# A transformer step on one core: the first feed-forward in seven half products, its adaLN vectors on TensorE

## The chip, the core and the metric

The kernel runs on one core of a Trainium2 chip. Its metric is the device time of one execution in microseconds (us). A core has five engines that run apart from each other: TensorE (PE in the profile, with PEld for its weight loads), VectorE (DVE), ScalarE (ACT), GpSimd (POOL) and SyncE (SP, which here only issues DMAs). Matmuls read SBUF and write PSUM, which has eight banks of 512 fp32 columns.

## What is computed

640 tokens (512 latent, 128 context) of width D = 1024 pass two layers. Layer 0 mixes tokens by neighbourhood attention, layer 1 by a gated linear recurrence (LRU); each is followed by a SwiGLU feed-forward of width 2816. Before every mixer and feed-forward stands an RMS norm with adaLN shift and scale, behind it a gated residual; these are six vectors per layer, for latent and context tokens each.

```python
def _adaln(cond, w_mod, b_mod):
    m = jax.nn.silu(cond) @ w_mod + b_mod            # 1024 x 6144 per layer
    return jnp.split(m, N_MOD, axis=-1)

def _modulate(x, g, shift, scale):
    return _rms_norm(x, g) * (1 + scale[:, None, :]) + shift[:, None, :]

def _swiglu(x, w_gu, w_down):
    gate, up = jnp.split(x @ w_gu, 2, axis=-1)
    return (jax.nn.silu(gate) * up) @ w_down
...
    ctx = ctx + g1_c[:, None, :] * o_c
    lat = lat + g1_l[:, None, :] * o_l
    f_c = _swiglu(_modulate(ctx, norm_g[i, 1], sh2_c, sc2_c), ffn_w_gu[i], ffn_w_down[i])
    f_l = _swiglu(_modulate(lat, norm_g[i, 1], sh2_l, sc2_l), ffn_w_gu[i], ffn_w_down[i])
    ctx = ctx + g2_c[:, None, :] * f_c
    lat = lat + g2_l[:, None, :] * f_l
```

## The kernel before

Activations lie transposed in SBUF: 8 blocks `k` of 128 features by 640 tokens. A product in fp32 precision is made of three fp32r matmuls: weights and activations are split into a high part (`whi`, `whx`, made by ScalarE's copy) and the rest (`wlo`, `wlx`, VectorE's difference), and hi·hi, hi·lo and lo·hi are added up in one PSUM bank. The function `some` issues them, L221 to L223, 24 for one output block of 128 features and one chunk of tokens (two chunks of 320, `CH`; 384 and 256, `CHL`, in the closing projections). Weights come by SP's DMA queue in pieces of 512 KB (`raw`).

The program is written once, and a scheduler that simulates the engines (`schedule_with_timeline_sim=True`) sets the order of each engine's instructions, within what tiles, pools (a tile waits until the buffer's earlier user is done) and pins (`issue_after`) allow. On the chip every engine then runs its own order and waits on semaphores.

The stages in order:

- `start`: the norm, the first two adaLN vectors and the first products of attention. The adaLN vectors are made on TensorE: with SiLU(cond) as 128 x 32 stationary block (`csp`, 2 columns used), four matmuls of 256 columns write four groups of 32 partitions of one bank (`ss`); the copied row is then turned into columns by matmuls with `sel`. `keep` issues dummy fp32 matmuls of 256 columns.
- `attn`: eight head pairs; `softmax` uses two PSUM banks `tp` for transpositions, two `sp` and one `op`. PE also gets products of the next pair, and the output projection's first ones.
- `ffn0`: the output projection of attention (`project` with `wo`), the moment (L540, L543) and the spread of its root (L557) of the norm, and `ffn`: for each of 22 columns of 128 features a gate and an up product, 2 x 2 chunks x 24 matmuls; the shift is a 2-column extra in one chunk (322 columns); after 8, 7 and 7 columns the down product, last in `project_closing`, which makes the LRU's input while it runs.
- `lru`, then `ffn1`: `project_halves` with `wlo`, and `ffn_halves`. Here x is kept in DRAM (`xd`), and the SBUF of x holds the normed activations as four blocks B11, B12, B21, B22 (half of the features by half of the tokens). Three columns are `plain`, the other 19 take gate and up products together by a Strassen form: seven products of 4 blocks x 3 matmuls x 320 columns (L1079 to L1081, in `product`), from sums of weights (`sum_weights`, POOL) and of activations (`sums`). The last down product is `project_last`.

The other ten adaLN vectors come from `modulations`, a generator of steps: `mod_cols` loads 128 rows of `w_mod` (512 KB, `mraw`, two buffers, POOL's DMA queue) and has VectorE multiply and add them up against `csb`, twice per load (L250, 1024 elements each). `fill(n)` takes n steps, at most the phase's `quota`; 24 are taken in attention and 56 in `ffn0`. `need` takes steps until a vector is there.

Of the kernel before, what the change touches and what calls it, by code (L numbers as in the profile page):

```python
# [36 lines left out]
FG = (1, 1, 1)  # L37
# [14 lines left out]
def _lay(inp):  # L52
# [30 lines left out]
    def tiles(w):  # L83
# [10 lines left out]
        "wm": wm.reshape(2, D, 6, D).transpose(0, 2, 3, 1).reshape(12, KT, P, D)[2:],  # L94
# [31 lines left out]
class _Step:  # L126
# [25 lines left out]
    def phase(self, name, **tags):  # L152
        with self.tc.tile_pool(name="ps" + name, bufs=1, space=bass.MemoryType.PSUM, reuse_waits="tile") as self.pp, \
                self.tc.tile_pool(name=name, bufs=1, reuse_waits="tile") as self.sb:
            self.wx, self.quota = [tags.pop(t, 0) for t in ("wx", "quota")]
            self.ptags, self.pbufs, self.share = list(tags), tags, True
# [139 lines left out]
    def start(self, hi, lo, sp, big):  # L296
# [5 lines left out]
        csp = self.t([P, KT, 32], F32, "csp", 1, sp)  # L302
# [91 lines left out]
        dve(nc.vector.tensor_scalar, v, aux[:, 256:256 + NT], 1.0 / D, EPS, ALU.mult, ALU.add)  # L394
# [5 lines left out]
        vectors(0, pm, 1, 1)  # L400
        row = rows(0, pm)
# [40 lines left out]
        keep(2)  # L442
# [109 lines left out]
    def spread(self, moment):  # L552
        nc = self.nc
        t0, bl, dg = moment
        ps = self.ps("rr" if "rr" in self.ptags else "mx")
# [35 lines left out]
    def project(self, w, hi, lo, gk, nxt=None, done=None, ahead=False):  # L591
        G = self.need(self.gcols, gk)
        for f in range(KT):
            u = self.unit(w[f], "m" if ahead else None)
            for t0, t1 in CH:
                self.residual(f, t0, t1, self.chunk(u, hi, lo, t0, t1, not ahead or f > 1), G, nxt)
                if nxt:
                    self.scale(f, t0, t1, *nxt)
            if done:
                done(f)  # L600
        if nxt:
            self.stats()
            self.shift(*nxt)

    def project_closing(self, w, hi, lo, gk, key, nh, nl, xd):
        G = self.need(self.gcols, gk)
        A, B = [self.need(self.AB, key + (j,)) for j in range(2)]
        us = []

# [4 lines left out]
        def normed(k, t0, t1):  # L614
            v = self.t([P, 384], F32, "nv", 3, self.sb)
# [3 lines left out]
        for f in range(KT):  # L619
            us.append(self.unit(w[f]))  # L620
            for c, (t0, t1) in enumerate(CHL):
                if c == 0 or f < KT - DEH:
                    out(f, t0, t1)
# [857 lines left out]
```

## Time and profile before

| | us |
|---|---|
| device time, median of 3 runs | 1521.38 (1519.66 to 1524.26) |
| device time of the profiled execution | 1522.34 |
| its span, first to last instruction | 1520.6 |
| PE busy | 1491.0 |
| DVE busy | 1062.4 |
| ACT busy | 697.9 |
| POOL busy | 253.2 |

The span is what the trace covers; the profiled execution's device time is 1.7 us more. Times in the trace count from the span's start. Matmuls overlap: one of 320 columns lasts 312 ns in the trace while the next starts some 147 ns after it, so a matmul's price in a full stretch is the distance of starts, not its duration. fp32 matmuls (not fp32r) stand as two entries each. The first feed-forward runs from about 372 to 863 us, the second from 1068 to 1510 us.

### The profile page before, as it was taken

The page shows a single profiled execution, that of the slowest core. Times are in us where ns is not written, and L with a number is a line of the kernel's source. Part 1 is how long each engine was busy: PE and PEld are TensorE (multiplying, and loading weights), DVE is VectorE, ACT ScalarE, POOL GpSimd, SP SyncE. Part 2 cuts the span into 40 slices and gives each one's busy share as a digit, 9 for nine tenths or more (in the row PEclk, how much of TensorE's full clock was granted, in tenths as well). Part 3 has the DMA queues.
Part 4 walks back from the last instruction along what each step waited for, and adds up shares of the span by engine and source line. Part 5 has one row for each costly group of instructions (what it writes and reads, how often), then busy time and mean ns, then how long its engine had stood idle before and what let it go on. Part 6 is the DMA issues. An engine that isn't in the chain of part 4 may idle for free. (4 is left out here: it accounts for less than half of the span.)

```text
span 1520.6 us, 26091 instructions
## 1 busy us (share of the span) xinstructions
PE 1491.0 (98%) x10359; PEld 1443.9 (95%) x10359; DVE 1062.4 (70%) x2005; ACT 697.9 (46%) x1268; POOL 253.2 (17%) x276
## 2 busy tenths in 40 slices
PE   8999999899999999999999999999999999999997
PEld 6999999899999999999999888899999999999997
DVE  5778998769999987434443769985965656566555
ACT  4576666754332123312321478864634342434243
POOL 0112132100111110000000114220322323222211
PEclk9999999999999999999999999999999999999999
DMA  9545665336566664222222443335342231323211
GB/s 379 165 142 162 188 188 172 117 136 187 179 190 197 207 195 134 62 84 84 65 64 92 145 131 109 119 104 175 97 125 83 71 111 56 100 67 98 70 56 70
DMA packets 72330, 196.65 MB, mean 129 GB/s; under 512 B 8048, under 2 KB 24592, under 8 KB 72080
## 3 DMA queue, kind: packets, MB, share of 16 engines
q1 hardware_dynamic: 57392, 142.32, 29.7%
q0 software_dynamic: 14240, 51.98, 11.2%
q8 instruction: 81, 1.33, 0.4%
q10 hardware_dynamic: 576, 0.68, 0.1%
q14 instruction: 41, 0.34, 0.1%
HBM read 179.48 MB, written 8.92 MB: 124 GB/s over the span
## 5 line engine op out<-in xcount | busy, mean ns | idle before, releaser
L221 PE MATMUL mm<-big,whi 128*128 128x320 f32 (+3 forms) x1233 | 383.7, 313 | 6.5 <-ACT big L1307 5.3
L222 PE MATMUL mm<-big,whi 128*128 128x320 f32 (+3 forms) x1233 | 383.7, 312 | 0.4 <-DVE big L564 0.2
L223 PE MATMUL mm<-big,wlo 128*128 128x320 f32 (+3 forms) x1233 | 383.9, 312 | 0.0
L221 PEld LDWEIGHTS mm<-big,whi 128*128 128x128 f32 x1233 | 232.8, 189 | 9.2 <-ACT big L1307 6.0
L222 PEld LDWEIGHTS mm<-big,whi 128*128 128x128 f32 x1233 | 233.3, 189 | 2.8 <-DVE big L1309 0.7
L223 PEld LDWEIGHTS mm<-big,wlo 128*128 128x128 f32 x1233 | 232.9, 189 | 1.5
L250 DVE SCALAR_TENSOR_TENSOR mprod<-mraw,csb 128x1024 f32<-128x1024 f32 x160 | 195.1, 1219 | 12.3 <-DMA mraw<-in_wm 11.8
L587 DVE SCALAR_TENSOR_TENSOR x<-mm,G,x 128x320 f32<-128x320 f32 (+2 forms) x192 | 77.9, 436 | 83.7 <-PE mm L223 83.5
L180 ACT CAST whi<-raw 128x1024 fp32r<-128x1024 f32 (+1 forms) x71 | 73.9, 1041 | 108.6 <-PE mm L222 62.4
L182 DVE TENSOR_TENSOR wlo<-raw,whi 128x1024 fp32r<-128x1024 f32 (+1 forms) x87 | 106.0, 1219 | 21.6 <-ACT whi L180 12.5
L221 PE MATMUL mm<-big,whx 128*128 128x320 f32 (+3 forms) x348 | 108.3, 311 | 0.0
L223 PE MATMUL mm<-big,wlx 128*128 128x320 f32 (+3 forms) x348 | 108.0, 310 | 0.0
L222 PE MATMUL mm<-big,whx 128*128 128x320 f32 (+3 forms) x348 | 107.8, 310 | 0.0
L246 POOL DMA_DIRECT2D mraw<-in_wm x80 | 43.1, 538 | 364.8 <-DVE mprod L250 270.5
L221 PE MATMUL mx<-big,whi 128*128 128x320 f32 (+3 forms) x287 | 89.4, 311 | 0.0
L223 PE MATMUL mx<-big,wlo 128*128 128x320 f32 (+3 forms) x287 | 89.1, 311 | 0.0
L222 PE MATMUL mx<-big,whi 128*128 128x320 f32 (+3 forms) x287 | 88.9, 310 | 0.0
L221 PE MATMUL mx<-big,whx 128*128 128x320 f32 (+3 forms) x260 | 80.6, 310 | 0.0
L223 PE MATMUL mx<-big,wlx 128*128 128x320 f32 (+3 forms) x260 | 80.5, 310 | 0.0
L180 ACT CAST whx<-raw 128x1024 fp32r<-128x1024 f32 (+1 forms) x40 | 41.1, 1029 | 85.5 <-PE mm L222 47.9
L222 PE MATMUL mx<-big,whx 128*128 128x320 f32 (+3 forms) x260 | 80.3, 309 | 0.0
L1307 ACT CAST whi<-raw 128x1024 fp32r<-128x1024 f32 (+1 forms) x41 | 41.3, 1008 | 73.2 <-PE mm L222 44.9
(347 smaller groups left out, 3721.5 us busy)
## 6 DMA issues: line engine op xcount, KB each, us to landing
raw<-in_gu SPq DMA_DIRECT2D x88, 512.0 KB, 3.5
mraw<-in_wm POOLq DMA_DIRECT2D x80, 512.0 KB, 3.9
raw<-in_dn SPq DMA_DIRECT2D x24, 512.0 KB, 3.6
sw<-in_wm SPq DMA_DIRECT2D x16, 512.0 KB, 10.7
raw<-in_wqk SPq DMA_DIRECT2D x16, 512.0 KB, 5.0
raw<-in_wi SPq DMA_DIRECT2D x16, 512.0 KB, 3.6
whi<-in_wi POOLq DMA_DIRECT2D x16, 512.0 KB, 4.1
raw<-in_dn SPq DMA_DIRECT2D x16, 448.0 KB, 3.3
```

What stands on the lines that cost most here:

```text
L180: nc.scalar.copy(hi, raw)
L182: nc.vector.tensor_tensor(lo, raw, hi.bitcast(F32), ALU.subtract)
L221: nc.tensor.matmul(ps, hi[:, k], xhi[:, k, s], start=(k == 0), stop=False)
L222: nc.tensor.matmul(ps, hi[:, k], xlo[:, k, s], start=False, stop=False)
L223: self.done = nc.tensor.matmul(ps, lo[:, k], xhi[:, k, s], start=False, stop=(k == last)).ins
L246: nc.gpsimd.dma_start(w, self.i["wm"][l * 6 + j - 2, f])
L250: nc.vector.scalar_tensor_tensor(prod, w, 1.0, self.csb[:, s], ALU.mult, ALU.mult, accum_out=out[:, s, f:f + 1])
L587: self.nc.vector.scalar_tensor_tensor(xs, ps[:, a - t0:b - t0], G[:, s, f:f + 1], xs, ALU.mult, ALU.add)
L1307: self.nc.scalar.copy(hi, v)
```

## The change

The first feed-forward takes the second one's code. `layer_end` is the old end of the program as a function, called for both layers: x is loaded, `project_halves` projects (for layer 0 its first five chunks as they come, `ahead`), writes x to DRAM and makes the four blocks, `ffn_halves` runs 3 plain columns and 19 in seven half products; its last down product is `project_closing` for layer 0, with weights loaded two at a time, chunk by chunk, and `project_last` for layer 1. `ffn` and `project` are gone.

Of the ten later adaLN vectors the first three stay on VectorE. The other seven are `mod_product`: 8 pieces of 512 KB each (`mraw`, two buffers, now on SP's queue), each with four 256-column matmuls into four groups of 32 partitions of one bank (L291), then a copy of the row, two matmuls that turn it (L297), and one addition that gives gate, shift or scale. Steps are taken by `fill` in `plain` and, three per column, in `ffn_halves`. In the start stage seven more dummies are issued, and the norm's sums are written 32 columns wide.

```diff
-FG = (1, 1, 1)
+FG = 3
...
     def modulations(self):
         yield from self.mod_gate(0, 2)
         yield from self.mod_ss(0, 3, 1)
-        yield from self.mod_gate(0, 5)
-        yield from self.mod_ss(1, 0, 0)
-        yield from self.mod_ss(1, 3, 1)
-        yield from self.mod_gate(1, 2)
-        yield from self.mod_gate(1, 5)
+        vecs = [(0, 5), (1, 1), (1, 0), (1, 2), (1, 4), (1, 3), (1, 5)]
+        srcs = [self.i["wmp"][l * 6 + j - 5, k] for l, j in vecs for k in range(KT)]
+        ahead = []
+
+        def piece():
+            while srcs and len(ahead) < 2:
+                w = self.t([P, D], F32, "mraw", 2, self.sb)
+                self.nc.sync.dma_start(w, srcs.pop(0))
+                ahead.append(w)
+            return ahead.pop(0)
+        for l, j in vecs:
+            yield from self.mod_product(l, j, piece)
+
+    def mod_product(self, l, j, piece):
+        nc = self.nc
+        ps = self.ps()
+        for k in range(KT):
+            w = piece()
+            for g in range(4):
+                nc.tensor.matmul(ps[32 * g:32 * g + 32, 0:256], self.csp[:, k], w[:, 256 * g:256 * g + 256], start=(k == 0), stop=(k == KT - 1))
+            if k < KT - 1:
+                yield
+        row = self.t([P, 256], F32, "row", 1, self.sb)
+        nc.scalar.copy(row, ps[:, 0:256])
+        for c in range(2):
+            nc.tensor.matmul(ps[:, 256 + 8 * c:264 + 8 * c], row[:, c * P:c * P + P], self.ident.rearrange("p (g c) -> p g c", g=4)[:, :, 0:2], start=True, stop=True)
...
+        nc.vector.tensor_tensor(out.rearrange("p s (g c) -> p s g c", c=2), ps[:, 256:272].rearrange("p (c g s) -> p s g c", c=2, g=4), b, ALU.add)
...
         pm = self.ps("ss")
+        keep(2)
         vectors(0, pm, 0, 0)
+        keep(2)
         vectors(0, pm, 0, 1)
         for j, b in enumerate(blocks):
-            pe(aux[:, 256 + j:257 + j], self.ssq[:, b:b + P], self.ones[:, 0:1], start=True, stop=True)
+            pe(aux[:, 288 + 32 * j:320 + 32 * j], self.ssq[:, b:b + P], self.ones[:, 0:32], start=True, stop=True)
...
         vectors(0, pm, 1, 1)
+        keep(2)
         row = rows(0, pm)
...
-        keep(2)
+        keep(3)
         normed(0)
...
-    def project_halves(self, w, hi, lo, gk, key, xd):
+    def project_halves(self, w, hi, lo, gk, key, xd, ahead=False):
...
+        if ahead:
+            for n, (f, t0, t1) in enumerate(early):
+                out(f, t0, t1, self.chunk(us[f], hi, lo, t0, t1, n > 2))
+            early = []
...
                 n += 1
+                self.fill(c or n > 2)
...
                 if f < PLAIN:
                     continue
+                self.fill(FG)
...
-        with self.phase("ffn0", at=2, rr=1, mx=2, wx=2, quota=56) as fp:
-            self.project(i["wo"], ohi, olo, (0, 2), ((0, 1), xhi, xlo), None, True)
...
-            self.ffn(0, xhi, xlo, fp, last)
+        mpool.close()
+        xd, xe = [dram.tile([D, NTOK], F32, tag=n, name=n) for n in ("xd", "xe")]
+        self.layer_end(xpool, i["x"], ohi, olo, i["wo"], 0, xd, True,
+                       lambda w, hi, lo, gk: self.project_closing(w, hi, lo, gk, (1, 0), xe))
...
-        with self.phase("ffn1", at=1, mx=3, mc=1, wx=2) as fp:
+        with self.phase(f"ffn{l}", at=1, mx=3, mc=1, wx=2, quota=0 if l else 56) as fp:
...
-            self.project_halves(i["wlo"], yhi, ylo, (1, 2), (1, 1), xd)
+            self.project_halves(w, hi, lo, (l, 2), (l, 1), xd, ahead)
```

Three places show how PE's order changes. In the rows a line number is that of each kernel's own file: L221 to L223 before are L222 to L224 after, L1079 to L1081 are L1067 to L1069, the moment's L540 and L543 are L576 and L579, the spread's L557 is L593; a number behind a name tells apart tiles of one tag, and the last figures are the output's size.

First, PE at the end of attention's output projection, ahead of the first feed-forward. Before, the projection's last product into an `mx` bank is followed by the moment of the norm:

```order
L221 MATMUL mx_4750<-big_4092,whx_4715 128x320
L222 MATMUL mx_4750<-big_4093,whx_4715 128x320
L540 MATMUL at_4673<-ones_72,ssq_4141 128x128
L540 MATMUL at_4691<-ones_72,ssq_4141 128x128
L543 MATMUL at_4691<-ones_72,sq_4635 128x128
L540 MATMUL at_4691<-ones_72,ssq_4141 128x128
L543 MATMUL at_4691<-ones_72,sq_4635 128x128
```

After:

```order
L224 MATMUL mm_4634<-big_3856,wlo_4399 128x320
L291 MATMUL tp_3201<-mraw_4839,csp_78 32x256 x4
L291 MATMUL tp_3201<-mraw_4872,csp_78 32x256 x4
L291 MATMUL tp_3201<-mraw_4906,csp_78 32x256 x4
L291 MATMUL tp_3201<-mraw_4939,csp_78 32x256 x4
L291 MATMUL tp_3201<-mraw_5021,csp_78 32x256 x4
L291 MATMUL tp_3201<-mraw_5054,csp_78 32x256 x4
L297 MATMUL tp_3201<-ident_63,row_5106 128x8 x2
L222 MATMUL mx_4294<-big_3856,whx_4290 128x320
L223 MATMUL mx_4294<-big_3857,whx_4290 128x320
```

Six pieces of the vector (0, 5) and its turn have come in between two products of the projection. The tile `tp` they add up in was taken in attention, from head pair 5 on: the step that `need` takes there to finish the third vector begins the fourth. Its bank is one of the two `tp` banks of attention and, in `ffn0`, the second `mx` bank.

Second, PE inside the first feed-forward, at the change from one product to the next. Before (`mx` and `mm` are banks of gate and up products):

```order
L223 MATMUL mx_5934<-big_4711,wlo_5931 128x320
L221 MATMUL mx_5934<-big_4711,whi_5930 128x320
L222 MATMUL mx_5934<-big_4712,whi_5930 128x320
L223 MATMUL mx_5934<-big_4711,wlo_5931 128x320
L221 MATMUL mm_5960<-big_4711,whi_5930 128x320
L222 MATMUL mm_5960<-big_4712,whi_5930 128x320
L223 MATMUL mm_5960<-big_4711,wlo_5931 128x320
L221 MATMUL mm_5960<-big_4711,whi_5930 128x320
```

After, in the seven half products (`mx_5623` and `mx_5774` are the accumulated halves of two columns):

```order
L1069 MATMUL mx_5623<-big_4722,wlx_5667 128x320
L291 MATMUL at_5610<-mraw_5750,csp_78 32x256 x4
L1068 MATMUL mx_5774<-big_4104,whi_5770 128x320
L1069 MATMUL mx_5774<-big_4104,wlo_5771 128x320
L291 MATMUL at_5610<-mraw_5756,csp_78 32x256 x4
L1067 MATMUL mx_5774<-big_4104,whi_5770 128x320
L1068 MATMUL mx_5774<-big_4104,whi_5770 128x320
L1069 MATMUL mx_5774<-big_4104,wlo_5771 128x320
```

Single pieces stand between fp32r matmuls, at 39 places in all for the last six vectors: 27 with one piece or part of one, 12 with two.

Third, PE at the spread of the norm's root ahead of the first feed-forward (`rr` before, a bank `mx` after). Before, 44 rows behind the moment:

```order
L222 MATMUL mm_4816<-big_4093,whi_4779 128x320
L223 MATMUL mm_4816<-big_4092,wlo_4780 128x320
L221 MATMUL mm_4816<-big_4092,whi_4779 128x320
L557 MATMUL rr_4686<-dg_4684,ones_72 128x128 x3
L222 MATMUL mm_4816<-big_4093,whi_4779 128x320
L223 MATMUL mm_4816<-big_4092,wlo_4780 128x320
```

After:

```order
L579 MATMUL at_4468<-ones_72,sq_4464 128x128
L576 MATMUL at_4468<-ones_72,ssq_4165 128x128
L579 MATMUL at_4468<-ones_72,sq_4464 128x128
L593 MATMUL mx_4481<-dg_4479,ones_72 128x128 x3
L222 MATMUL mx_4486<-big_3856,whi_4135 128x320
L223 MATMUL mx_4486<-big_3857,whi_4135 128x320
```

The spread now stands directly behind its moment.

More of the change, by code (lines that the diff above doesn't have):

```diff
@@ L589, in residual, with project_closing @@
             self.square(f, t0, t1)
[L591 to L605, printed above, removed]
+    def project_closing(self, w, hi, lo, gk, key, xd):
         G = self.need(self.gcols, gk)
@@ L608, in project_closing @@
         us = []
+        for f in range(0, KT, 2):
+            us += self.two(w[f:f + 2], f % 4)
+        nh, nl = self.nh, self.nl = [self.big(n=NTOK + 2) for _ in range(2)]
         def out(f, t0, t1):
@@ L619, in project_closing @@
         for f in range(KT):
[L620 to L623, printed above, removed]
-        for c, (t0, t1) in enumerate(CHL):
-            for f in range(KT - DEH, KT) if c else ():
-                out(f, t0, t1)
-                j = f - KT + DEH
-                for k in range(max(0, 2 * j - 2), 2 * j) if f < KT - 2 else ():
+            out(f, *CHL[0])
+        self.stat(*CHL[0])
+        for f in range(KT):
+            out(f, *CHL[1])
+            if 2 < f < KT - 1:
+                for k in range(2 * f - 6, min(2 * f - 4, 6)):
                     normed(k, *CHL[0])
-            for k in (6, 7) if c else ():
-                normed(k, *CHL[0])
-            self.stat(t0, t1)
+        for k in (6, 7):
+            normed(k, *CHL[0])
+        self.stat(*CHL[1])
         for k in range(KT):
@@ L998, in sums @@
         t2 = self.t([P, HT], F32, "c22", 2, self.sb)
-        nc.vector.tensor_tensor(b11, b12, b11, ALU.subtract)
+        with self.pin(self.halved):
+            nc.vector.tensor_tensor(b11, b12, b11, ALU.subtract)
         nc.vector.tensor_tensor(t2, b22, b11, ALU.subtract)
```

92 lines of the change are left out of this document (32 added, 60 removed).

## The prediction

> **What bounds the kernel now.** I read the page's first lines first: which engine fills the span.
>
> ```profile
> span 1520.6 us, 26091 instructions
> ...
> PE 1491.0 (98%) x10359; PEld 1443.9 (95%) x10359; DVE 1062.4 (70%) x2005; ACT 697.9 (46%) x1268; POOL 253.2 (17%) x276
> ```
>
> TensorE is busy for 98% of it. That share is pipelined, so I next cut the span into stages: window, then busy us and instructions of PE, PEld, DVE, ACT and POOL, then granted clock, DMA share and GB/s.
>
> ```profile
> 16.00:20.00 4.00, 3.16 (x26) 2.40 (x19) 1.13 (x4) 1.56 (x2) 1.19 (x1) 0.70 1.03 420
> 20.00:24.00 4.00, 4.00 (x16) 3.34 (x14) 2.49 (x8) 1.70 (x3) 0.00 (x0) 0.50 1.03 413
> 290.00:300.00 10.00, 5.83 (x44) 5.09 (x44) 7.99 (x14) 9.50 (x18) 1.69 (x3) 0.71 0.38 109
> 290.00:326.00 36.00, 29.90 (x246) 27.11 (x245) 23.56 (x64) 22.53 (x50) 2.29 (x5) 0.91 0.27 86
> 396.00:846.00 450.00, 450.00 (x3054) 450.00 (x3053) 292.72 (x532) 120.23 (x224) 25.33 (x47) 1.00 0.42 129
> 846.00:870.00 24.00, 21.04 (x137) 19.64 (x136) 19.00 (x53) 13.62 (x33) 2.04 (x9) 1.00 0.38 116
> 1068.00:1116.00 48.00, 46.24 (x309) 45.82 (x308) 42.19 (x78) 27.35 (x63) 13.24 (x9) 0.96 0.35 104
> 1116.00:1486.00 370.00, 369.74 (x2506) 368.79 (x2505) 218.16 (x348) 140.74 (x227) 99.79 (x72) 1.00 0.27 82
> ```
>
> The reader is to see two saturated stretches: 396 to 846 (first feed-forward) and 1116 to 1486 (second). They make one matmul per 450/3054 = 0.1473 us and per 370/2506 = 0.1476 us, nearly all with 320 columns. There is no idle PE time in the first, so there the count of PE work alone sets the time. The list of waits for PE alone (who waited for what: us in total, times, longest) names the two stalls that the prediction uses:
>
> ```profile
> PE at L540 <- DVE ssq L527: 1.7, 1, 1.7
> PE mm L1137 <- DVE xt L1309: 1.8, 1, 1.8
> ```
>
> VectorE's adaLN products in that stretch:
>
> ```profile
> 396.00:846.00 450.00, 111.66 (x182) 1.00 0.42 129
> ```
>
> These 111.7 us of VectorE go away, but VectorE is busy 292.7 of 450 us and no PE wait stands in the stretch: their removal is worth nothing by itself. What it buys is room for the weight sums.
>
> **The change, part by part.** The sum is made on PE time and taken against the profiled span of 1520.6 us (device time 1522.3; the three other runs have the median 1521.4, 0.9 us below it). Three runs spread over 0.3%, about what can be told from no change.
>
> *Seven half products.* Of 22 columns, 3 stay plain and 19 need 7 x 4 x 3 = 84 matmuls of 320 columns where they had 2 x 2 x 24 = 96. 19 x 12 = 228 fewer, at 0.1475: **-33.6 us**. The down products keep their number; the moved split of the last one (384+256 for 320+320 columns) is neutral. The second feed-forward shows that the form runs unstalled at the same rate (369.7 of 370 us), with its sums hidden under 218 us of VectorE.
>
> *Seven vectors on TensorE.* The first stage has the same instruction (four 32x256 groups, a piece), between the same kind of matmul; the columns are start, us, engine, line and what.
>
> ```profile
> 27.40 0.31 PE L318 MATMUL kk<-big,whi 128*128 128x320 f32 x1
> 27.64 0.64 PE L318 MATMUL ss<-sw,csp 128*32 128x256 f32 x8
> 28.21 0.42 PE L318 MATMUL mm<-big,whi 128*128 128x320 f32 x1
> 28.46 0.31 PE L318 MATMUL kk<-big,whi 128*128 128x320 f32 x1
> ...
> 37.49 0.31 PE L318 MATMUL kk<-big,whi 128*128 128x320 f32 x1
> 37.73 1.93 PE L318 MATMUL ss<-sw,csp 128*32 128x256 f32 x32
> 39.59 0.42 PE L318 MATMUL mm<-big,whi 128*128 128x320 f32 x1
> 39.84 0.31 PE L318 MATMUL kk<-big,whi 128*128 128x320 f32 x1
> ```
>
> Without the piece the matmul of 28.46 would start 2 x 0.147 after that of 27.40; it starts 1.06 after: a lone piece costs 0.77 us. Four in a row cost 39.84 - 37.49 - 0.29 = 2.06, so a further one costs 0.43 and each run of pieces 0.33 for going into the narrow form and back. The PE order has the last six vectors' 48 pieces in 39 runs, 51 parts since three are split: 39 x 0.33 + 51 x 0.43 = **+34.8 us**. They stand between matmuls that leave no gap, so nothing hides them. That alone eats the saving. Bounds: 24 runs of two (28.6) and 51 lone parts (39.3).
>
> *Turning a vector* (two matmuls of a copied row) is nearest to the first stage's four:
>
> ```profile
> 32.64 0.31 PE L318 MATMUL kk<-big,wlo 128*128 128x320 f32 x1
> 32.89 1.05 PE L318 MATMUL at<-sel,row 128*128 128x2 f32 x8
> 33.80 0.39 PE L318 MATMUL mm<-big,wlo 128*128 128x320 f32 x1
> 34.03 0.31 PE L318 MATMUL kk<-big,wlo 128*128 128x320 f32 x1
> ```
>
> 34.03 - 32.64 - 0.29 = 1.1 for four, 0.55 for two. Six vectors: **+3.3** (0, if the copy's wait is an idle that pieces use, to 6.6).
>
> *The first vector.* Two of its pieces run in attention (a switch or two more, +1, down to 0: 290 to 326 has 6.1 us idle). The other six and the turn stand in one block, ahead of the output projection's `mx` products; there are two `mraw` buffers. Two pieces lie ready, the third can be fetched only once the first is used, the fifth only after the third. The landings of `mraw`:
>
> ```profile
> DMA to landing us min/median/max: 3.6/3.9/7.0
> ```
>
> So 0.6, then 3.9 and a piece, again 3.9 and a piece, the row copy and the turn: 0.6 + 4.4 + 4.4 + 0.5 + 1.1 = **+11 us** in which PE has little else, because its order is fixed. Bounds: 3.5 (everything ready: 0.33 + 6 x 0.43 + 0.55) and 18 (landings of 7.0). Behind the waiting pieces stand all products of the projection's first half, its moment and norm; SP's queue holds the next weights behind the fetches, but those are wanted some 20 us later.
>
> An idle PE also loses its clock:
>
> ```profile
> 296.40 0.90 PE L221 MATMUL mm<-big,whi 128*128 128x320 f32 x2 [3.23 <-ACT big L1307]
> ```
>
> After 3.23 us idle the stretch 290 to 300 ran at 0.71: 2.9 us of clock in 10. Two waits of 3.9: **+1.5**, between 0 and 2.9. The Trainium skill, "TensorE: Matmul & The Clock Gate", Part 1, says that an idle window of about 3.4 us halves the clock until PE has been busy as long again; by it this term would be about 1.7. The rows agree.
>
> *The moment and the spread.* In the new order the spread's matmuls follow their moment at once, where 44 rows lay between. What passes between them is seen in the second layer:
>
> ```profile
> 1049.42 0.39 PE L543 MATMUL at<-ones,sq 128*128 128x128 f32 x2
> ```
> ```profile
> 1050.36 0.15 DVE L545 TENSOR_SCALAR var<-at 128x3 f32<-128x3 f32 x1
> 1051.52 0.56 DVE L549 TENSOR_TENSOR dg<-ident,rs 128x384 f32<-128x384 f32 x1 [1.00 <-POOL rs L547]
> ```
>
> 1051.52 + 0.56 less 1049.42 + 0.39: PE will wait **+2.3 us** (0 if both lie under another wait, 4 with a busy VectorE).
>
> *The halves of the normed x* bring the second layer's wait on `xt`, **+1.8** (0 to 3).
>
> *Attention with one transposition bank.* The first vector holds one of two `tp` banks from pair 5 on, so each later transposition waits for the copy before it:
>
> ```profile
> ACT PT L841 <- PE tp L839: 21.2, 20, 2.6
> ```
>
> ACT waits for PE at these copies now, not PE for ACT; 18 are left. **+1** (0, to 5.4: nine copies of 0.6 in the last pair). A gain has no source there.
>
> *Fetches on SP's queue.* `mraw` moves from POOL's queue to SP's, where a fetch waits for its buffer with weights queued behind it. By the PE order at least 5.3 us of PE work lie between the use of a piece and that of the piece two later, in 31 of 47 cases 7.5; a landing takes 3.6 to 7.0. **+2**, nearer the median landing; 0 to 15 (1.0 in each of the 16 tight cases).
>
> *First-stage dummies.* 7 more `keep`s:
>
> ```profile
> 34.48 0.69 PE L318 MATMUL at<-csp,ident 128*128 128x256 f32 x2
> 35.31 0.41 PE L318 MATMUL mm<-big,whi 128*128 128x320 f32 x1
> ```
>
> 0.83 us each on a warm PE, some in waits for DMA and for the row; they are to end the 7 us at 0.70 and 0.50 in 16 to 24, which cost at most 3.7 us. **-1** (-3 to +3). The five 32-column sums cost nothing visible beside them.
>
> *The closing projection* puts a chunk between each moment and spread; 846 to 870 has 3.0 us idle. **-1** (-3 to 0). x through DRAM, the pools and `K` move DMAs off PE's path: 0, under the second layer's 82 GB/s.
>
> Sum: -33.6 + 34.8 + 3.3 + 1 + 11 + 1.5 + 2.3 + 1.8 + 1 + 2 - 1 - 1 = **+23.1 us**: span 1543.7, device 1545.4, median **1544.5 us**.
>
> **Rivals.** (1) *Pieces that cost no PE time*, if the array takes them in the gaps of the half form. The 38.1 us of pieces and turns go: 1506. It decides from 23 of the 38 hidden. For it: a PE that waits more has room. Against: 369.7 busy of 370 in that form. (2) *The first vector does not wait*: its fetches run ahead, since the block's first two come early. Then 3.5 for 11, no lost clock, and the spread alone: +14, 1536; with the dummies and the closing at their best, 1531. For it: DMA share 0.42 there. Against: two buffers. (3) *SP's queue becomes the bound* of the first feed-forward: pieces late, and weights behind pieces late, at the 16 tight places and the doubles: +13 over my 2, 1557. For it: landings up to 7.0 against 5.3. Against: median 3.9. (4) *No change to measure*: piece runs at the lower bound (-6), the block at 3.5 with no clock lost (-9), dummies and closing at their best (-4): 1525.
>
> **How the numbers follow.** Forecast 0.52, (2) 0.17, (3) 0.14, (1) 0.08, (4) 0.09. Faster is (1): 0.08; (4) gives within 0.3%: 0.09; slower 0.83. The range leaves out (1) and what lies beyond (3): 1524 to 1561.
>
> **What would show it.** Right: about 7116 - 7032 = 84 fewer 320-column matmuls in all, piece runs with 0.77 between the matmuls around them, a PE wait on DMA `mraw` of some 8 us near the first layer's projection with a clock under 1.0 there, and a first feed-forward a little longer than before, at 1.00 clock, with VectorE idler. Wrong: piece runs that cost 0.4 or less, a first feed-forward 25 us shorter, or PE waits on `raw` or `mraw` all through it.

## The result, and the profile after

The changed kernel takes 1568.9 us (median of 4 runs, 1565.2 to 1569.5) against 1522.8 us: ratio 1.030, 95% interval 1.0273 to 1.0325. On another occasion it took 1565.1 us against 1523.0: 1.028 (1.0259 to 1.0295). So it is slower by 42 to 46 us. The forecast was +23.1, and the time lies above the range. The direction was right; the size was not.

The page's first lines after:

```profile
span 1567.7 us, 26797 instructions
...
PE 1512.1 (96%) x10621; PEld 1427.2 (91%) x10621; DVE 1012.6 (65%) x1881; ACT 750.3 (48%) x1335; POOL 335.8 (21%) x300
```

The span grew by 47.1 us and PE's busy time by 21.1, so 26 us are new idle time. The stretches of the changed kernel show where it lies (same columns as in the prediction):

```profile
290.00:333.00 43.00, 33.22 (x248) 27.47 (x246) 26.25 (x70) 25.36 (x53) 3.65 (x6) 0.92 0.37 120
333.00:364.00 31.00, 30.28 (x187) 30.28 (x188) 11.35 (x21) 4.97 (x8) 0.00 (x0) 0.89 0.42 136
364.00:382.00 18.00, 9.99 (x72) 5.63 (x71) 2.08 (x4) 1.42 (x2) 0.00 (x0) 0.68 0.64 215
382.00:440.00 58.00, 52.48 (x364) 51.18 (x364) 43.05 (x94) 32.97 (x75) 11.64 (x6) 0.98 0.22 78
440.00:860.00 420.00, 419.43 (x2990) 393.95 (x2989) 230.67 (x374) 153.72 (x249) 105.09 (x78) 1.00 0.44 140
```

The feed-forward itself (440 to 860) is as full as before, at full clock. Some 18 of the 26 us of new idle time stand ahead of it, at the end of attention and in the output projection; the rest lies in later stages. The waits of PE in the changed kernel, the longest first:

```profile
PE tp L291 <- DMA mraw<-in_wmp: 7.5, 4, 3.6
PE mx L593 <- DVE dg L585: 4.1, 3, 1.9
PE mm L222 <- ACT big L1297: 3.9, 3, 1.6
...
PE mm L223 <- DVE big L1299: 3.1, 2, 1.6
PE tp L861 <- ACT PT L863: 2.6, 5, 0.8
PE at L576 <- DVE ssq L563: 2.5, 1, 2.5
```

In the kernel before, the longest sums are 5.3 us for ACT's splits (`big`, 3.2 of it within attention) and 2.4 for a softmax tile. The waits for `mraw`, of a transposition for the copy before it (`PT` L863) and for the spread's `dg` (L585) are new; VectorE's splits (`big` L1299) were waited for 0.2 us before. The wait for `ssq` was 1.7 us in the closing projection and is 2.5 in the output projection. The places, by the starts of the same PE instructions in both profiles:

| stage, by PE instructions | before, us | after, us | difference |
|---|---|---|---|
| start to the last value projection (in attention) | 265.1 | 264.1 | -1.0 |
| from there to attention's last product | 59.4 | 65.5 | +6.1 |
| to the first gate product of the recurrent stage | 551.5 | 587.1 | +35.6 |
| first to last gate product | 110.9 | 115.3 | +4.4 |
| to the end | 533.7 | 535.7 | +2.1 |

The third row holds the projection and the first feed-forward: there the 320-column products saved 34 us and some 69 us came in. The block of the first vector, in PE's order of time:

```profile
365.51 0.31 PE L224 MATMUL mm<-big,wlo 128*128 128x320 f32 x1
365.75 1.07 PE L291 MATMUL tp<-mraw,csp 128*32 128x256 f32 x16
370.40 1.08 PE L291 MATMUL tp<-mraw,csp 128*32 128x256 f32 x8 [3.58 <-DMA mraw<-in_wmp]
372.07 1.08 PE L291 MATMUL tp<-mraw,csp 128*32 128x256 f32 x8 [0.59 <-DMA mraw<-in_wmp]
375.97 1.08 PE L291 MATMUL tp<-mraw,csp 128*32 128x256 f32 x8 [2.82 <-DMA mraw<-in_wmp]
377.58 1.08 PE L291 MATMUL tp<-mraw,csp 128*32 128x256 f32 x8 [0.53 <-DMA mraw<-in_wmp]
379.15 1.02 PE L297 MATMUL tp<-ident,row 128*128 128x8 f32 x4 [0.49 <-ACT row L295]
380.02 0.61 PE L222 MATMUL mx<-big,whx 128*128 128x320 f32 x1
380.43 0.47 PE L223 MATMUL mx<-big,whx 128*128 128x320 f32 x1
...
383.63 0.47 PE L223 MATMUL mx<-big,whx 128*128 128x320 f32 x1
```

It lasts 14.3 us, with the two long waits for a fetch that were forecast. Behind it 0.41 us pass from the first product's start to the next and then 0.267, 13 times, instead of 0.147: 1.8 us more, the granted clock being 0.50 up to 384 us and 1.00 from there:

```profile
380.00:384.00 4.00, 4.00 (x16) 4.00 (x17) 0.17 (x1) 0.00 (x0) 0.00 (x0) 0.50 0.43 135
384.00:388.00 4.00, 4.00 (x29) 4.00 (x28) 2.01 (x3) 1.78 (x3) 0.00 (x0) 1.00 0.11 41
```

The second place is the start of the projection:

```profile
329.15 0.71 PE L939 MATMUL op<-PT,cv 128*64 128x128 f32 x8
331.48 0.71 PE L222 MATMUL mm<-big,whi 128*128 128x320 f32 x3 [1.62 <-ACT big L1297]
333.72 0.63 PE L223 MATMUL mm<-big,whi 128*128 128x320 f32 x1 [1.54 <-DVE big L1299]
334.15 0.47 PE L224 MATMUL mm<-big,wlo 128*128 128x320 f32 x1
```

PE waits for the last split of attention's output, and some 20 products behind the waits run at half clock (0.50 from 334 to 339 us), 2.5 us more. In the kernel before an `mx` product follows attention's last one at once, and PE does not wait:

```profile
324.19 0.61 PE L917 MATMUL op<-PT,cv 128*64 128x128 f32 x8
324.73 0.42 PE L221 MATMUL mx<-big,whi 128*128 128x320 f32 x1
```

The pieces in the feed-forward cost what the first stage had shown. These rows have half a piece (4 instruction records; a whole one has 8) and one and a half:

```profile
522.64 0.32 PE L224 MATMUL mm<-big,wlo 128*128 128x320 f32 x1
522.89 0.62 PE L291 MATMUL at<-mraw,csp 128*32 128x256 f32 x4
523.44 0.41 PE L1067 MATMUL mx<-xt,wuh 128*128 128x320 f32 x1
523.69 0.30 PE L1068 MATMUL mx<-xt,wuh 128*128 128x320 f32 x1
...
526.91 0.31 PE L1069 MATMUL mc<-big,wlx 128*128 128x320 f32 x1
527.15 1.06 PE L291 MATMUL at<-mraw,csp 128*32 128x256 f32 x12
528.14 0.42 PE L1067 MATMUL mx<-big,whx 128*128 128x320 f32 x1
528.40 0.31 PE L1068 MATMUL mx<-big,whx 128*128 128x320 f32 x1
```

523.69 - 522.64 - 0.295 = 0.76 for half a piece, as much as a whole one costs; 528.40 - 526.91 - 0.295 = 1.19 for two parts. In the feed-forward 38 such runs stand among 320-column products, 33.9 us in sum; the 39th, two pieces, stands between the moment and the spread, where PE has to wait in any case. The forecast had 34.8 for the 39.

### The profile page after: what moved, and what is told of

It reads as the page before. It is cut to its first block, busy times and chain, and to the rows that moved or that the text cites. A ratio compares the mean times of both kernels' runs of the same rounds, so it can differ in the third digit from the quotient of the medians.

```text
span 1567.7 us, 26797 instructions
## 1 busy us (share of the span) xinstructions
PE 1512.1 (96%) x10621; PEld 1427.2 (91%) x10621; DVE 1012.6 (65%) x1881; ACT 750.3 (48%) x1335; POOL 335.8 (21%) x300
## 5 line engine op out<-in xcount | busy, mean ns | idle before, releaser
L223 PE MATMUL mm<-big,whi 128*128 128x320 f32 (+2 forms) x1184 | 371.8, 314 | 6.4 <-DVE big L600 3.2
L222 PE MATMUL mm<-big,whi 128*128 128x320 f32 (+2 forms) x1184 | 370.2, 314 | 4.1 <-ACT big L1297 3.9
L224 PE MATMUL mm<-big,wlo 128*128 128x320 f32 (+2 forms) x1184 | 370.8, 314 | 0.0
L223 PEld LDWEIGHTS mm<-big,whi 128*128 128x128 f32 x1184 | 226.1, 191 | 10.7 <-DVE big L600 5.2
L222 PEld LDWEIGHTS mm<-big,whi 128*128 128x128 f32 x1184 | 224.9, 190 | 8.8 <-ACT big L1297 4.6
L224 PEld LDWEIGHTS mm<-big,wlo 128*128 128x128 f32 x1184 | 226.0, 191 | 1.2
L623 DVE SCALAR_TENSOR_TENSOR x<-mm,G,x 128x128 f32<-128x128 f32 (+3 forms) x283 | 114.5, 435 | 133.2 <-PE mm L224 132.7
L1299 DVE TENSOR_TENSOR wlo<-raw,whi 128x1024 fp32r<-128x1024 f32 (+1 forms) x82 | 103.6, 1264 | 44.3 <-ACT whi L1297 43.8
L1299 DVE TENSOR_TENSOR wlx<-sum,whx 128x1024 fp32r<-128x1024 f32 x76 | 98.4, 1295 | 51.9 <-ACT whx L1297 51.8
L1297 ACT CAST whx<-sum 128x1024 fp32r<-128x1024 f32 x76 | 79.7, 1049 | 87.5 <-POOL sum L1045 44.4
L1067 PE MATMUL mx<-big,whx 128*128 128x320 f32 x304 | 94.3, 310 | 0.0
L1067 PE MATMUL mc<-big,whx 128*128 128x320 f32 x304 | 94.2, 310 | 0.0
L1068 PE MATMUL mc<-big,whx 128*128 128x320 f32 x304 | 94.2, 310 | 0.0
L1069 PE MATMUL mc<-big,wlx 128*128 128x320 f32 x304 | 93.9, 309 | 0.0
L1068 PE MATMUL mx<-big,whx 128*128 128x320 f32 x304 | 93.7, 308 | 0.0
L1069 PE MATMUL mx<-big,wlx 128*128 128x320 f32 x304 | 93.7, 308 | 0.0
L1073 ACT COPY snap<-mx 128x320 f32<-128x320 f32 x114 | 46.1, 423 | 83.6 <-PE mx L1069 83.4
L183 DVE TENSOR_TENSOR wlo<-raw,whi 128x1024 fp32r<-128x1024 f32 x53 | 65.7, 1239 | 26.7 <-ACT whi L181 15.7
L1297 ACT CAST big<-g 128x320 fp32r<-128x320 f32 x88 | 40.4, 459 | 48.0 <-DVE g L1086 33.9
L1299 DVE TENSOR_TENSOR big<-g,big 128x320 fp32r<-128x320 f32 x88 | 50.8, 577 | 17.2 <-ACT big L1297 17.2
```

The source lines that it names most:

```text
L183: nc.vector.tensor_tensor(lo, raw, hi.bitcast(F32), ALU.subtract)
L222: nc.tensor.matmul(ps, hi[:, k], xhi[:, k, s], start=(k == 0), stop=False)
L223: nc.tensor.matmul(ps, hi[:, k], xlo[:, k, s], start=False, stop=False)
L224: self.done = nc.tensor.matmul(ps, lo[:, k], xhi[:, k, s], start=False, stop=(k == last)).ins
L623: self.nc.vector.scalar_tensor_tensor(xs, ps[:, a - t0:b - t0], G[:, s, f:f + 1], xs, ALU.mult, ALU.add)
L1067: nc.tensor.matmul(ps, hi[:, k], xh[:, k], start=start and k == 0, stop=False, skip_group_check=not start)
```

## Experiments

The theory after this reading: the 23 us beyond the forecast come from the first vector, which is begun inside attention. Beside its block, it holds a bank, and the bank is missed in two places. The rivals: the half form or the closing projection have stalls of their own; the pieces cost more than forecast.

**e1_late, the first vector begun in the feed-forward**

```diff
+        yield
         for l, j in vecs:
...
                     self.need(self.AB, (0, 1, 1))
+                    self.quota = 0
```

> The changed kernel, but its first vector begins only in the first feed-forward: no piece in attention, no bank of the transpositions held. Theory A (the held bank): beside the block of six pieces it costs the end of attention (each transposition waits for the copy before it) and the first products of the output projection, which lose the bank in which they would run ahead of the last split. Then this kernel takes back about 6 us in the attention's end, 4 us of wait and lost clock at the projection's start and 17 us of block and lost clock, and pays 8 more pieces and a turn among the half products, 6 us: about 1547 us (1543 to 1551), with no PE wait on mraw and an attention that ends within 1.5 us of where it did before. Rival: only the two waits of the block for DMA and the clock after them come back, 10 to 11 us: 1558 (1555 to 1561), with the attention's end as late as in the changed kernel.

1550.2 us (1548.8 to 1550.7) against 1523.3: 18.6 us less than the changed kernel (14.9 less than when that was measured again, in e5_again), in theory A's range. But A's split of it was partly wrong: attention's last product is at 327.4 us, only 2.2 us earlier than in the changed kernel and still 2.9 later than before. At the projection's start one wait of 1.2 us is left, and behind it PE has the full clock:

```profile
327.05 0.64 PE L940 MATMUL op<-PT,cv 128*64 128x128 f32 x8
327.62 0.42 PE L222 MATMUL mx<-big,whx 128*128 128x320 f32 x1
...
329.68 0.41 PE L224 MATMUL mx<-big,wlx 128*128 128x320 f32 x1 [1.21 <-DVE wlx L183]
```

The projection starts on an `mx` bank here, as before. In the changed kernel that bank belonged to the vector. In the feed-forward e1_late pays for 51 runs among 320-column products, 47.4 us by the starts (one of them with a 3.4 us wait for a fetch, which A had not expected), where the changed kernel pays for 38 and 33.9 us. So the vectors cost e1_late 13.5 us more there and not A's 6. As its first gate product comes 12.4 us earlier all the same, the early start costs about 26 us, near the 27 that A gives back; the rival has 10 to 11.

**e2_pairs, pieces two at a time**

```diff
-            if k < KT - 1:
+            if k % 2 and k < KT - 1:
                 yield
...
-FG = 3
+FG = 1
...
-quota=0 if l else 56
+quota=0 if l else 28
```

> As e1_late, but the pieces are issued two at a time: 39 runs of pieces on PE where e1_late has 52, as many pieces. If going into the narrow form and back costs 0.33 us a run beside 0.43 a piece (the prediction's price), 13 runs fewer give 4 to 5 us less than e1_late: about 1542. Rival: a piece costs its own time wherever it stands and the switch nothing that counts: the same as e1_late within 1.5 us.

1541.5 us (1539.3 to 1547.7), 8.7 less than e1_late. By the starts the 38 runs among 320-column products cost 41.1 us against 47.4, each sum with waits for a fetch (3.1 and 3.4 us). That is 13 runs fewer and, as fewer pieces are split, 57 parts against 63: 13 x 0.33 + 6 x 0.43 = 6.9, where the starts give 6.3. So the price of a run is confirmed. The rest of the difference lies in the second layer, whose order is the same in both (2.8 us from the recurrent stage's last gate product on), so it is most likely the difference of two executions.

**e3_few, one piece of eight**

```diff
-            for g in range(4):
+            for g in range(4 if k == 0 else 0):
```

> As e1_late, but of each vector's eight pieces only the first is multiplied; the other seven are still fetched (the vectors' values are wrong, nothing else is left out). Prediction's price: 49 pieces x 0.43 + 43 runs x 0.33 = 35 us less than e1_late, about 1512. Rival 1 (the pieces fit into gaps of the half form, so cost no PE time): within 3 us of e1_late. Rival 3 (SP's queue is the bound): hardly less than e1_late too, since all fetches are still there.

1518.7 us (1513.6 to 1521.5): 31.5 us less than e1_late, 3.5 short of the price's 35. In the feed-forward PE now waits 7.5 us for ScalarE and VectorE (the longest wait 3.9), which it does not in e1_late, and for no fetch. Both rivals fall: pieces do cost PE time, and the fetches, all of which are still there, are not the bound.

**e4_dve, half products with the vectors on VectorE**

```diff
-        for l, j in vecs:
-            yield from self.mod_product(l, j, piece)
+        for l, j in vecs:
+            yield from self.mod_rows(l, j)
...
+                w = self.t([P, D // 2], F32, "mraw", 2, self.sb)
+                nc.gpsimd.dma_start(w, self.i["wm"][l * 6 + j - 2, f][:, h * 512:h * 512 + 512])
+                    nc.vector.scalar_tensor_tensor(prod, w, 1.0, self.csb[:, s, h * 512:h * 512 + 512], ALU.mult, ALU.mult, accum_out=two[:, h, s, f:f + 1])
```

> Seven half products alone: the seven vectors go back to VectorE (as half rows of 512 elements, to find room in memory), none of their pieces on PE; closing projection, spread and dummies as in the changed kernel. Theory: what is left of the change is -33.6 for the 228 products and the waits that the changed kernel shows outside the pieces, +5 around the projection's moment, +4 in the closing projection, +4 in the recurrent stage, +2 in the second feed-forward, -1 at the start: about 1503 us (1497 to 1509). Rival: VectorE, 231 us busy in the 420 of the changed feed-forward, cannot take some 125 us of vectors more beside the halves' splits and becomes the bound there: 1515 or more, with PE waits on DVE all through it.

1558.5 us (1554.2 to 1560.6): the rival. The stretch of the half products, and PE's waits from 340 to 900:

```profile
440.00:800.00 360.00, 328.58 (x2137) 318.18 (x2136) 330.34 (x665) 118.82 (x193) 143.42 (x150) 0.99 0.44 139
```
```profile
PE mc L1082 <- DVE g L1093: 9.1, 9, 2.2
PE mm L221 <- DVE x L638: 9.1, 8, 2.4
PE mx L608 <- DVE dg L600: 5.3, 1, 5.3
```

VectorE is busy 330 of 360 us (198 of 360 in the changed kernel) and PE 329. The two halves of the change therefore do need each other: the half form leaves VectorE no room for the vectors, at least as half rows.

**e5_again, the changed kernel once more.** No edit.

> The changed kernel itself, unaltered, for a second profile. In its first one the recurrent stage (first to last gate product) took 115.4 us and what follows it 528.6, against 110.9 and 526.6 before and 111.1 and 526.2 in e1_late, whose order of instructions is the same from there on. If these 6.7 us belong to the first vector's start in attention (a knock-on through the fetches), they stand here again. If they are what one execution differs from the next, this profile shows 111 to 113 and 524 to 527, and the time moves with it: 1562 to 1566.

1565.1 us (1563.5 to 1567.3). The second profile has 110.1 us from the first to the last gate product and 534.4 from there to the end of its span (1562.1); the first had 115.3 and 535.7. Attention's last product is at 329.9 and the first gate product at 917.6, as in the first (329.6 and 916.6). So 6.6 us of the first profile's difference to before, in the two last stages, do not come again (the spans differ by 5.6); what lies ahead of the recurrent stage does.

**e6_hold and e9_hold, the bank alone**

e6_hold:

```diff
                     self.quota = 0
+                    hold = self.ps()
+                    nc.tensor.matmul(hold[:, 0:P], self.ident, self.ident, start=True, stop=True)
...
             self.split(ohi[:, KT - 1], olo[:, KT - 1], O[:, KT - 1])
+            nc.vector.tensor_copy(self.t([P, 1], F32, "held", 1), hold[:, 0:1])
```

> e1_late with one bank of the transpositions held, from pair 5 to the last split of attention, by a single 128-column product that is read at the end; the first vector still begins only in the first feed-forward, and nothing is held beyond attention. If the held bank by itself costs what the prediction gave it, 1 us (0 to 5.4): 1551 to 1553, with the last product of attention 2 us later than in e1_late at most. Rival: holding it costs the attention's end 5 us or more, since each transposition waits for a copy: 1556 or above. If 1551, the loss that e1_late took back lay in the block ahead of the output projection.

1552.9 us (1547.2 to 1553.7). It says nothing of the bank: the copy that ends the hold was moved forward to 268 us. e9_hold ties it to the last split:

```diff
-            self.split(ohi[:, KT - 1], olo[:, KT - 1], O[:, KT - 1])
-            nc.vector.tensor_copy(
+            done = self.split(ohi[:, KT - 1], olo[:, KT - 1], O[:, KT - 1])
+            with self.pin(done):
+                nc.vector.tensor_copy(
```

> e6_hold again, with the read of the held bank tied to the last split of attention: in e6_hold it had been moved forward to 268 us, so nothing was held there. Now all transpositions from pair 5 on use one bank. Prediction's price: 1 us (0 to 5.4), 1551 to 1555.5, last product of attention at 328 to 330 us. Rival: 5 us or more in attention, 1556 or above. The two profiles of the changed kernel, where the bank is held too, have that product at 329.6 and 329.9, e1_late has it at 327.4, so 2 to 2.5 us is the likeliest.

1559.3 us (1558.2 to 1559.6): 9.1 us more than e1_late, beyond the prediction's 5.4. My own figure for attention held (its last product is at 329.9, 2.5 us later), but not as the whole price; nor are the 5 us in attention, as the rival had it. By the projection's first moment it is 6.1 us behind e1_late, so 3.6 lie behind attention, with the same two waits at the projection's start as in the changed kernel and the half clock behind them:

```profile
331.90 0.71 PE L222 MATMUL mm<-big,whi 128*128 128x320 f32 x3 [1.61 <-ACT big L1298]
334.14 0.64 PE L223 MATMUL mm<-big,whi 128*128 128x320 f32 x1 [1.54 <-DVE big L1300]
```

The bank that attention calls `tp` is the one in which the projection would start an `mx` product. The first gate product comes 7.6 us later than in e1_late. What is added behind the projection is a longer wait for a fetch (`mraw`, 4.9 us here, 3.4 there; 2.1 us by the starts of that run of pieces), and no run shows that the bank causes it. So 6.1 us is what the bank shows by itself.

**e7_close, the closing projection's old order**

```diff
-        for f in range(KT):
-            out(f, *CHL[0])
-        self.stat(*CHL[0])
+        for f in range(KT):
+            for c, (t0, t1) in enumerate(CHL):
+                if c == 0 or f < KT - DEH:
+                    out(f, t0, t1)
...
```

> e1_late with the chunks of the closing projection in the order that the kernel before has (of the second chunk, two ahead of the first moment). The prediction gave the new order -1 us (-3 to 0). If that is right, this is 1 to 3 us slower than e1_late: 1552. Rival, from the changed trace, which has 4.9 us of waits for VectorE's and ScalarE's normalisation at the end of this projection where the kernel before has 3.7 us of waits in all: 1 to 3 us faster than e1_late, 1548.

1551.1 us (1550.5 to 1553.8), 0.9 from e1_late: neither. Its waits move (1.6 us ahead of the second moment, and shorter waits behind it), their sum hardly: 4.5 us up to the first gate product, 4.6 in e1_late.

**e8_three, vectors on VectorE, GpSimd and ScalarE**

```diff
+                    if s:
+                        nc.gpsimd.tensor_tensor(prod, w, c, ALU.mult)
+                        nc.scalar.activation(prod, prod, AF.Copy, accum_out=two[:, h, s, f:f + 1])
```

> e4_dve with half of the vectors' products moved from VectorE to GpSimd, with the sum over the row by ScalarE (a product of 512 elements on GpSimd, then an accumulating copy), and the rows fetched on SP's queue. VectorE then has some 85 us less to do in the first feed-forward (some 415 of 560 us instead of 500 of 573), GpSimd some 160 more, ScalarE some 70 more; TensorE has no pieces. Theory: what made e4_dve slow is VectorE alone; its waits fall from some 43 us to 10 or less: 1515 to 1525, near the kernel before or under it. Rival: GpSimd's weight sums, which stand in its order behind the products, come late and PE waits for these instead: 1535 or more.

1592.6 us (1591.8 to 1597.5), the slowest of all. VectorE was not relieved:

```profile
440.00:800.00 360.00, 307.23 (x1900) 293.11 (x1900) 321.98 (x492) 171.80 (x375) 251.72 (x158) 0.95 0.44 139
```
```profile
L293 DVE SCALAR_TENSOR_TENSOR at<-mraw,csb x112: 681/756/1848, 383.9 to 786.7; 128x512 f32<-128x512 f32 x112
```

It has half of the products and is busy 322 of 360 us: with GpSimd busy 252 us beside it, its instructions grew longer (last section). The run changes more than the engine: VectorE's products are written to a PSUM bank, and the rows come by SP's queue.

**e10_before_later, the kernel before without its vector's first row in attention**

```diff
+        yield
         yield from self.mod_gate(0, 5)
...
                     self.need(self.AB, (0, 1, 1))
+                    self.quota = 0
...
-        with self.phase("ffn0", at=2, rr=1, mx=2, wx=2, quota=56) as fp:
+        with self.phase("ffn0", at=2, rr=1, mx=2, wx=2, quota=60) as fp:
```

> The kernel before, with one thing changed: its first gate vector of the first layer's feed-forward, on VectorE, begins only in the first feed-forward (its first row was computed in attention). In all forms of the changed kernel without pieces in attention the last product of attention stands at 327 to 329 us, 3 us later than before. If the order of attention's end turned worse because that vector's rows left it, this kernel shows it too: 327 to 328 and 1525 to 1527. Rival: the new order comes from what follows (the other order of the projection's first chunks and its banks): 324 to 325.5, and 1523, as before.

1526.9 us (10 runs) against 1523.9, ratio 1.0019 (1.0004 to 1.0033); attention's last product at 327.1 us. The first expectation holds for this kernel: taking the rows out of attention is enough to end it 2.6 us later. It is not a fixed price, since e11_none (below), without any such rows, has the product at 325.2: the order of attention's end, which the scheduler makes anew in each kernel, is worth up to 3 us.

**e11_none, no vectors at all**

```diff
-            for g in range(4):
-                nc.tensor.matmul(ps[32 * g:32 * g + 32, 0:256], self.csp[:, k], w[:, 256 * g:256 * g + 256], start=(k == 0), stop=(k == KT - 1))
...
-        nc.vector.tensor_tensor(out.rearrange("p s (g c) -> p s g c", c=2), ps[:, 256:272].rearrange("p (c g s) -> p s g c", c=2, g=4), b, ALU.add)
+        nc.vector.tensor_copy(out.rearrange("p s (g c) -> p s g c", c=2), b)
```

> e1_late without any of the seven vectors' work: no fetch, no piece, no turn; the vectors hold their bias alone (that part of the computation is left out, on TensorE and on VectorE). It shows what the seven half products and the new closing projection give by themselves. By the products' count -33.6, and the waits that e1_late shows outside the pieces, +3 at attention's end, +3 around the moment, +2 in the closing projection: 1523 - 25.6 = 1497 (1493 to 1501). Rival: the half form in this layer has stalls of its own, which the pieces hide: 1505 or more.

1499.0 us (1498.1 to 1501.4) against 1523.9: -24.9, ratio 0.984 (0.9822 to 0.9856), inside the expected range. The half products do give most of their count, and their stretch is full; PE's waits from the projection to the closing are few:

```profile
400.00:800.00 400.00, 399.24 (x2701) 398.12 (x2700) 242.57 (x387) 153.89 (x253) 116.61 (x81) 1.00 0.30 89
```
```profile
PE mm L223 <- DVE big L592: 3.1, 4, 1.2
PE mx L585 <- DVE dg L577: 2.1, 1, 2.1
PE mx L224 <- DVE wlx L183: 1.2, 1, 1.2
```

From the experiments, in medians: -24.9 (e11_none against before) + 51.3 (e1_late against e11_none: seven vectors among the products) + 14.9 to 18.6 (the changed kernel against e1_late: the first vector begun in attention) = +41.3 to +45.0. These are steps between the same medians, so the sum has to come near the measured +42.2 to +46.1; what it shows is the shares.

No version here that does the whole computation beats the kernel before (e3_few and e11_none leave out part of it). The nearest, e2_pairs, is 18 us slower. The 56 pieces alone, without a single change of form and without turns, are 56 x 0.43 = 24 us of PE, and the half form gives 24.9.

## Why the prediction was too low

*Seven half products, -33.6: right in the count.* 7116 - 7032 = 84 fewer 320-column matmuls stand in the profile, as forecast, and the feed-forward stays full. With the small terms that belong to them (spread +2.3, `xt` +1.8, fetches +2, dummies -1, closing -1) the forecast without vectors is -29.5; e11_none has -24.9. The spread's wait is there as forecast (2.1); the wait on `xt` and the cost of the fetches are not. In their place stand 1.2 us at the projection's start, 1.3 at attention's end, and waits of 3.6 us in the closing projection that follow on 3.0 before. Another 3 us are half clock that the kernel before does not have in these places: by the distances of starts 1.1 us behind the spread's wait and some 2 in the closing projection. There e11_none has a clock of 0.52 in the stretch below, where the kernel before has 1.00 from 846 to 870 us:

```profile
824.00:831.00 7.00, 5.79 (x18) 4.92 (x19) 6.45 (x14) 2.60 (x7) 0.00 (x0) 0.52 0.30 102
```

The forecast had no clock term for the spread or the closing projection. The terms for dummies and closing can't be told from nothing: kernels without the new dummies start attention's first score product (`sp`) at 72.3 us (e10_before_later) and 73.7 us (before), kernels with them at 72.5 (e4_dve) to 74.3 us (e8_three), and e7_close moves nothing. The bound of 3.7 us behind the dummies' term was also added up wrongly: the two rows from 16 to 24 us give 4 x 0.30 + 4 x 0.50 = 3.2.

*Pieces +34.8 and turns +3.3: right.* 33.9 for 38 runs, with the 39th in a wait, and, by the starts, 2.7. That the 39th would lie in the spread's wait was not forecast.

*Fetches on SP's queue +2 (rival 3): too high.* The changed kernel has no wait for `mraw` outside the block (0.2 us in its second profile), and e3_few, with all fetches, is fast. But the forms that begin the first vector later (e1_late, e2_pairs, e7_close, e9_hold) wait 3.1 to 4.9 us for one or two fetches.

*First vector, +11 and lost clock +1.5: the block itself was near, the clock too small.* 14.3 us with waits for DMA of 7.5, and 1.8 us at half clock behind it. Inside the 14.3 four of the six pieces ran at half clock too, 1.08 us each where a piece at full clock takes 0.64: another 1.8. The two long waits were near the forecast's 3.9; the waits of 0.59 and 0.53 for each pair's second piece were missing. The clock's price was taken from a stretch in attention in which PE waits anyway; in and behind the block there is work. The reading of that stretch was off as well: the clock was down to 0.50 from 294.1 us on, 0.9 us into the wait that ends at 296.4, so it did not fall after 3.23 us idle.

*One transposition bank, +1 (0 to 5.4): the step that failed.* e9_hold puts it at 6.1 us by the projection's first moment, 2.5 in attention and 3.6 behind it (by the medians at 9.1, with other waits). I priced what the bank does in attention, 18 transpositions. I did not ask who takes the bank next: the projection's product, which covers the last split. Its place was in the order: the block stands ahead of the `mx` products because it holds their bank, and I used that for the block only.

*The moment and the spread, +2.3: too low in the changed kernel.* There PE waits 5.6 us around the projection's first moment and spread (2.5 for `ssq`, 2.3 for `dg`, 0.8 for `var`), in e1_late 1.0. The wait for `ssq` was at nothing in the forecast.

Bank (6.1), block (14.3), the clock behind it (1.8) and the pieces in attention (1.4: 0.76 and 0.65 for two runs, a third is hidden in a wait) make 23.6 us, where the forecast had 14.5. The profiles alone give more: up to the recurrent stage the changed kernel is 12.4 us behind e1_late, which itself pays 13.5 more for the vectors' pieces and 0.4 for its turn, 26.3 in sum; the longer waits around the moment are the likeliest rest. So the first vector missed by 11.8 us. This, the 4.6 of the half form without vectors, and the 5.6 by which the first profile differs from the second make 22 of the 23 us by which the first measurement lies over the forecast. No single term carries the miss: the bank's share is 5.1 us. The rivals were all about the pieces and their fetches; none had the bank, so the range ended too low.

Where those 5.6 us come from is open: the recurrent stage runs the same order with 110 or 115 us, and in the longer one VectorE waits 3.9 us for a weight buffer at 996 us, in the shorter one 1.3. It was not tried further.

## What to carry to other kernels

A buffer or bank held across the end of a stage is to be priced by its next owner too: list who takes it next, and what that work covers. A saving of matmuls that is paid for with another engine's relief should be weighed as one sum first: here 25 us of products cost at least 24 us of pieces before any change of form. Narrow matmuls put between wide ones are best given out in whole groups, since half a piece cost as much as a whole one.

## What was not expected of the hardware

The half clock came without a long wait. Stretches of the changed kernel around the end of attention:

```profile
320.00:324.00 4.00, 1.88 (x14) 1.27 (x13) 2.50 (x11) 3.16 (x9) 0.00 (x0) 1.00 0.27 36
324.00:327.00 3.00, 1.86 (x14) 1.39 (x16) 0.00 (x0) 1.90 (x4) 0.00 (x0) 0.82 1.01 396
327.00:330.00 3.00, 2.86 (x32) 2.62 (x28) 0.09 (x1) 0.95 (x2) 0.00 (x0) 0.61 1.03 404
...
334.00:339.00 5.00, 5.00 (x20) 5.00 (x21) 3.20 (x6) 2.14 (x4) 0.00 (x0) 0.50 0.88 289
```

From 320 to 327 PE is busy 3.7 of 7 us, with waits of at most 0.77 us each, most of them of a transposition for the copy before it; the clock is at 0.82 on average from 324 to 327 and at 0.61 behind. The Trainium skill, "TensorE: Matmul & The Clock Gate", Part 1, gives an idle window of about 3.4 us as the cause of a drop, and in its section on a second failure mode says that frequent short idles do it too. The rows here agree with the second; no wait here is 3.4 us long.

In e8_three VectorE's products of 512 elements took from 681 to 1848 ns, and in e4_dve from 671 to 2221 ns. What sorts them is whether a GpSimd addition or product runs at the same time: in e4_dve the 163 products without one took 671 to 695 ns, the 61 with one 1280 ns on average; in e8_three the 17 without took 681 to 701 ns, the 95 with one 1130 on average. The Trainium skill, "Perfetto Trace Analysis", section "Optimizing Scalar/DVE Operations", says that GpSimd and VectorE share a read port, so moving work between them might not help; e8_three agrees: 112 products fewer on VectorE, and 34 us slower than e4_dve.

Going from 128-wide to 32-wide matmuls and back cost 0.33 us each time, even for a quarter of a piece (0.74 us in e1_late). Full-width fp32 matmuls of 128 columns between the same products show no such fixed part: one transposition (two records) costs 0.22 us there, two cost 0.44. So it goes with the narrow form; what in that form takes the time, no run separates. The Trainium skill, "TensorEngine Tiling (Array Packing)", Key Properties, says that a change of the tiling mode drains TensorE; it gives no number.
